# Up projection by Strassen's seven products, with part of its weight sums made by adding DMAs, and a down projection in two passes

## The chip, the cores and the metric

The kernel runs on one core of a Trainium2 chip. The core has five engines that take their instructions from queues of their own and in order: TensorE (PE in the profile; its weight loads are listed as PEld), VectorE (DVE), ScalarE (ACT), GpSimd (POOL) and SyncE (SP, which here only issues DMAs). The time is the device time of one execution in microseconds; lower is better. Runs of this kernel lie within about 0.2% of each other.

## The reference

One decoder block on a sequence of 512 tokens with D_MODEL = 2048, batch 1, everything float32:

```
mod = silu(c) @ w_ada + b_ada                      # six shift/scale/gate vectors
h   = rmsnorm(x) * (1 + sc1) + sh1
p   = h @ w_in                                     # input projection, 4384 columns
mix = concat(rwkv7_mixer(p[:, :3360]), pool_mixer(p[:, 3360:])) @ w_out
x   = x + gt1 * mix
h   = rmsnorm(x) * (1 + sc2) + sh2
u   = h @ w_up                                     # 2048 x 11264: 44 value and 44 gate tiles of 128
y   = causal depthwise conv of width 3 over u, plus bias
x   = x + gt2 * ((silu(y_gate) * y_value) @ w_down)   # 5632 x 2048
out = rmsnorm(x)
```

The change touches the last third: the second norm, `w_up`, the convolution, `w_down`. The rest keeps its arithmetic.

## The kernel before

Activations are kept transposed: channels on the 128 partitions, the 512 tokens along the free dimension. So a matrix of 2048 rows is 16 blocks of 128 (`KT`), and an output tile of 128 channels is one bank of the accumulation memory, 128 x 512 float32.

Every large matmul is made of three. A float32 operand is split into a high part, rounded to the fast format `F32R`, and a low part, the remainder; `mm3` (L111) then adds high x high, high x low and low x high into the same bank. Weights are split as they arrive: `split_weights` (L102) issues a DMA of 128 x 512 on SP (`wraw`, four buffers), ScalarE writes the high part (`whi`, L106), VectorE subtracts (`wlo`, L108; three buffers each). `project` (L116) runs this over the blocks of one output tile: 16 blocks for a tile of the up projection, 48 matmuls of 512 columns. The result of splitting activations lies in `ah`/`al` (L131) or, for the second norm, in `H2` (`hh`/`hl`).

Behind the two mixers the order of the work is as follows.

1. The output projection with `w_out` (L743 to L774). The last six output tiles are done in two halves of 256 tokens (`out_half`, L759), so that the second norm of the first half (`norm_rows`, `norm_bcast`, `second_norm`) can be computed while the second half is multiplied. Here GpSimd takes some of the weight splits.
2. `up_first` (L735): the first four column tiles of the up projection, block by block for one half of the tokens and then the other, with the rest of the second norm beside it.
3. Six groups of 8, 8, 8, 8, 4 and 8 pairs (`GROUPS`, L29). For each pair, `up_tile` (L813) makes a value and a gate tile, `conv` (L818) reads them from the bank (one ScalarE and two VectorE instructions each), then come Silu, a product, and `split_act`. When a group is complete, its activations are multiplied with the group's columns of `w_down` for all 16 output tiles, and added to the residual `x2` in SBUF (L848). In the first group VectorE also computes the 16 columns of the last gate (`ada_gate2`, L804), in four quarters each.
4. In the last group the output tiles 8 to 15 are again done in two halves (`down_half`, L856), with the final norm and the stores of the first half beside the second (L866 to L884).

The order of instructions on each engine comes from a scheduler in the framework, which places them by its own cost estimates and by dependences; the program order is its starting point. DMAs wait in the order in which SP issues them: a DMA that waits for its buffer holds up those behind it.

Of the kernel before, what the change touches and what calls it, by code (L numbers as in the profile page):

```python
# [16 lines left out]
P = 128  # L17
# [8 lines left out]
NWF = 8  # L26
Q = float(np.exp(-0.5))
WINS = (2, 4, 8, 16)
GROUPS = (8, 8, 8, 8, 4, 8)  # L29
# [25 lines left out]
def block_kernel(ctx, tc, a, out, stop=None, dbg=None):  # L55
# [4 lines left out]
    actp = ctx.enter_context(tc.tile_pool(name="act", bufs=1))  # L60
    wp = ctx.enter_context(tc.tile_pool(name="wts", bufs=2))
# [3 lines left out]
    cmat = cp.tile([P, 5, P], F32, tag="cmat", name="cmat")  # L65
    nc.sync.dma_start(cmat, a["cmat"][:, :, :])
    ident, bones, bmean, cent, ones = (cmat[:, i, :] for i in range(5))
    masks = cp.tile([P, 4, P], F32, tag="masks", name="masks")
    nc.sync.dma_start(masks, a["mask4"][:, :, :])
    mlev = cp.tile([P, 2, 64], F32, tag="mlev", name="mlev")  # L70
    nc.sync.dma_start(mlev, a["mlev"][:, :, :])
    scanm = cp.tile([P, NC, 129], F32, tag="scanm", name="scanm")
    nc.gpsimd.memset(scanm, 1.0)
    nc.gpsimd.memset(scanm[:, :, 0:1], 0.0)
    lanei = cp.tile([64, 16, 16], F32, tag="lanei", name="lanei")
    nc.sync.dma_start(lanei, a["lanei"][:, :, :])
    prec = cp.tile([P, 16], F32, tag="prec", name="prec")
# [33 lines left out]
    def mm3(ps, wh, wl, xh, xl, start, stop):  # L111
        PE.matmul(ps, wh, xh, start=start, stop=False)  # L112
        PE.matmul(ps, wh, xl, start=False, stop=False)  # L113
        return PE.matmul(ps, wl, xh, start=False, stop=stop)  # L114
# [575 lines left out]
    HT = T // 2  # L690

# [6 lines left out]

    def sumsq(acc, src, lo, hi, fresh):
        if fresh:  # L700
            S.activation(acc[:, lo:hi], src, AF.Square)
        else:
            t = rb.tile([P, T], F32, tag="h2", name="sqx", bufs=2)
            S.activation(t[:, lo:hi], src, AF.Square)
            V.tensor_add(acc[:, lo:hi], acc[:, lo:hi], t[:, lo:hi])

    H2 = [(rb.tile([P, T], F32R, tag=f"hh{k}", name=f"hh{k}"), rb.tile([P, T], F32R, tag=f"hl{k}", name=f"hl{k}"))
          for k in range(KT)]

    def residual(f, ps, gate, acc, lo, hi, fresh):  # L710

        V.scalar_tensor_tensor(x2[f][:, lo:hi], ps, gate, x2[f][:, lo:hi], op0=ALU.mult, op1=ALU.add)
        sumsq(acc, x2[f][:, lo:hi], lo, hi, fresh)
# [11 lines left out]
    def second_norm(hf, rstd, k):  # L725
        hs = slice(hf * HT, (hf + 1) * HT)
        t = rb.tile([P, T], F32, tag="h2", name="h2", bufs=2)[:, 0:HT]
        hi, lo = H2[k]
        modulate(hi[:, hs], lo[:, hs], t, x2[k][:, hs], rstd, gsc2[:, k : k + 1], mod[:, 48 + k : 49 + k])

    def up_first(hf, k):
        hs = slice(hf * HT, (hf + 1) * HT)
        wh, wl = split_weights(a["wup0"][k, :, :], G if hf == 0 and k % 2 else V)
        for i in range(4):
            sl = slice(i * P, (i + 1) * P)  # L735
            mm3(ups[i][:, hs], wh[:, sl], wl[:, sl], H2[k][0][:, hs], H2[k][1][:, hs], start=k == 0, stop=k == KT - 1)

    acc = rb.tile([P, T], F32, tag="acc", name="acc")
    x2 = []
    for k0 in range(4, KT, 4):  # L740
        for i in range(k0, min(k0 + 4, KT - 2)):
            load_mix(i)
        if k0 == KT - 4:  # L743
            M += last_mix
        for f in range(8):
            out_block(f, k0)
            if k0 == 8:
                for i in range(2):
                    t = rb.tile([P, T], F32, tag=f"x2_{2 * f + i}", name=f"x2_{2 * f + i}")
                    nc.sync.dma_start(t, a["xT"][:, 2 * f + i, :])  # L750
                    x2.append(t)
    for f in range(8):
        residual(f, pss[f], mod[:, 32 + f : 33 + f], acc, 0, T, f == 0)
    for f in range(8, NW):
        ps = bank()
        project(ps, a["wout"][f, :, :], M)
        residual(f, ps, mod[:, 32 + f : 33 + f], acc, 0, T, False)

    def out_half(hf, f, engs=(V,)):  # L759
        ps = bank()[:, 0:HT]  # L760
        project(ps, a["wout"][f, :, :], half(M, hf), engs=engs)
        residual(f, ps, mod[:, 32 + f : 33 + f], acc, hf * HT, (hf + 1) * HT, False)

    for f in range(NW, KT):
        out_half(0, f)
    for f in range(NW, KT):
        if f == NW + 1:
            dg = norm_rows(acc[:, 0:HT])
        if f == NW + 2:
            rstd0 = norm_bcast(dg)  # L770
        if f >= NW + 2:
            for k in range(3 * (f - NW - 2), 3 * (f - NW - 1)):
                second_norm(0, rstd0, k)
        out_half(1, f, (V, G) if f >= NW + 2 else (V,))  # L774

    ups = [bank() for _ in range(4)]
    for k in range(KT):
        if k + 12 < KT:
            second_norm(0, rstd0, k + 12)
        if k == 2:  # L780
            dg = norm_rows(acc[:, HT:T])
        if k == 5:
            rstd = norm_bcast(dg)
        if k >= 5:
            for k_ in range((k - 5) * 2, min((k - 4) * 2, KT)):
                second_norm(1, rstd, k_)
        up_first(0, k)
    for k in range(KT):
        up_first(1, k)
# [4 lines left out]
    def slot(i, dt=F32):  # L794
        return actp.tile([P, T], dt, tag=f"a{'hl'[i // 16]}{i % 16}", name="slot")

    cbs = []
    for i in range(4):
        t = slot(8 + i)
        nc.sync.dma_start(t, cact[0:1, i * T : (i + 1) * T].partition_broadcast(P))  # L800
        cbs.append(t)
    modg = cp.tile([P, 4, KT], F32, tag="modg", name="modg")

    def ada_gate2(j, after):  # L804
        for kq in range(4):
            wa = slot(12 + (4 * j + kq) % 4)
            nc.sync.dma_start(wa, a["ada2"][kq, 48 + j, :, :])
            jk = slot(24 + (4 * j + kq) % 2)
            with tc.issue_after(after.ins):
                V.scalar_tensor_tensor(jk, wa, 1.0, cbs[kq], op0=ALU.mult, op1=ALU.mult,  # L810
                                       accum_out=modg[:, kq, j : j + 1])

    def up_tile(n):  # L813
        ps = bank()
        project(ps, a["wup"][n, :, :], H2)
        return ps

    def conv(ps, j, tag):  # L818
        y = rb.tile([P, T], F32, tag=tag, name=tag, bufs=2)
        S.activation(y, ps, AF.Identity, bias=col("cb", j), scale=col("cw", 176 + j))  # L820
        V.scalar_tensor_tensor(y[:, 1:T], ps[:, 0 : T - 1], col("cw", 88 + j), y[:, 1:T], op0=ALU.mult, op1=ALU.add)
        V.scalar_tensor_tensor(y[:, 2:T], ps[:, 0 : T - 2], col("cw", j), y[:, 2:T], op0=ALU.mult, op1=ALU.add)
        return y

    j0 = 0
    for gi, gn in enumerate(GROUPS):
        A = []
        for jj in range(gn):
            j = j0 + jj
            yv = conv(ups[2 * j] if j < 2 else up_tile(2 * j), j, "t0")  # L830
            yg = conv(ups[2 * j + 1] if j < 2 else up_tile(2 * j + 1), 44 + j, "t1")
            S.activation(yg, yg, AF.Silu)
            after = V.tensor_mul(yv, yv, yg)
            A.append(split_act(jj, yv))
            if gi == 0 and jj >= 4:
                for i in range(4 * (jj - 4), 4 * (jj - 3)):
                    ada_gate2(i, after)
        if gi == 0:
            V.tensor_add(modg[:, 0, :], modg[:, 0, :], modg[:, 1, :])
            V.tensor_add(modg[:, 2, :], modg[:, 2, :], modg[:, 3, :])  # L840
            V.tensor_add(modg[:, 0, :], modg[:, 0, :], modg[:, 2, :])
            V.tensor_add(mod[:, 80:96], modg[:, 0, :], cols("b_ada", 80, 96))
        wsrc = a["wdn"][:, :, j0 * P : (j0 + gn) * P]
        if gi < len(GROUPS) - 1:
            for f in range(KT):
                ps = bank()
                project(ps, wsrc[f], A)
                V.scalar_tensor_tensor(x2[f], ps, mod[:, 80 + f : 81 + f], x2[f], op0=ALU.mult, op1=ALU.add)  # L848
        else:

            acc = rb.tile([P, T], F32, tag="acc", name="acc")

            def gate(f):
                return mod[:, 80 + f : 81 + f]

            def down_half(hf, f):  # L856
                ps = bank()[:, 0:HT]
                project(ps, wsrc[f], half(A, hf))
                residual(f, ps, gate(f), acc, hf * HT, (hf + 1) * HT, False)

            def finish(hf, k, rstd):
                hs = slice(hf * HT, (hf + 1) * HT)
                V.scalar_tensor_tensor(x2[k][:, hs], x2[k][:, hs], col("nf", k), rstd, op0=ALU.mult, op1=ALU.mult)  # L863
                nc.sync.dma_start(out[:, k, hs], x2[k][:, hs])
# [119 lines left out]
```

## Time and profile before

| what | value |
|---|---|
| median of three runs | 2449.82 us (2446.82 to 2450.76) |
| the profiled execution | 2452.14 us, of which the span from first to last instruction is 2450.0 |
| granted clock of TensorE, mean | 0.992 |
| busy: TensorE, VectorE, ScalarE, GpSimd | 2347.1, 1408.7, 874.6, 23.7 us |
| moved by DMA | 352.61 MB, mean 144 GB/s |

A group line of the profile reads: source line, engine, operation, output <- inputs, shapes, count | busy time in us, mean ns of one | idle time of the engine just before them, and who ended it. Busy times of matmuls overlap (their ends are modelled), so the cost of a matmul in a stream is read from the distance of starts or from counts in a window, not from its mean. A window line gives a stretch of time and each engine's busy time and count in it.

### The profile page before, as it was taken

How to read it: one execution, taken by the hardware profiler on the slowest of the kernel's cores; microseconds unless marked ns; L12 is line 12 of the kernel's file. 1: busy time of each engine (PE TensorE's matmuls, PEld its weight loads, DVE VectorE, ACT ScalarE, POOL GpSimd, SP SyncE). 2: the span in 40 equal slices, each digit the busy share in tenths (PEclk: the TensorE clock that was granted, in tenths of full speed). 3: DMA queues.
4: the chain of work that ended last, by engine and by line, in shares of the span. 5: the costliest groups of instructions: out<-in, count | busy, mean ns of one | idle time of the engine just before them, and what ended most of it. 6: DMA issues, size and time to landing. Idle time of an engine off the chain costs nothing.

```text
span 2450.0 us, 36089 instructions
## 1 busy us (share of the span) xinstructions
PE 2347.1 (96%) x13714; PEld 1872.0 (76%) x13714; DVE 1408.7 (57%) x2698; ACT 874.6 (36%) x1402; POOL 23.7 (1%) x29
## 2 busy tenths in 40 slices
PE   4889999999999999999999999999999999999997
PEld 3656666667667889887888888888888888888887
DVE  7987677787774357757534443444344434444457
ACT  3244443443433336532223322333233323323333
POOL 0000000000000002100000000000000000000000
PEclk9999999999999999999999999999999999999999
DMA  9975564556662635538533333333332333332335
GB/s 353 337 233 152 166 185 140 163 162 178 169 200 85 203 111 185 181 113 260 161 96 98 96 98 95 99 96 98 95 99 95 99 95 99 95 99 95 99 97 174
DMA packets 232160, 352.61 MB, mean 144 GB/s; under 512 B 74865, under 2 KB 80177, under 8 KB 227761
## 3 DMA queue, kind: packets, MB, share of 16 engines
q1 hardware_dynamic: 231986, 350.30, 46.0%
q8 instruction: 107, 1.75, 0.3%
q14 instruction: 67, 0.55, 0.1%
HBM read 334.22 MB, written 16.00 MB: 143 GB/s over the span
## 4 chain that ended last, share of the span: by engine, by line
PE 68%; DMA 3%; DVE 2%; ACT 1%; issue 0%; SPq 0%; POOL 0%; DVEq 0%; ACTq 0%; POOLq 0%
PE b L112 20%; PE b L114 20%; PE b L113 20%; DMA wraw<-wup 1%; PE mm L112 1%; PE mm L113 1%; PE mm L114 1%; DMA war<-ada 0%; PE pa L290 0%; DMA slot<-ada 0%; DMA wraw<-wdn 0%; DVE wlo L108 0%; DVE x L863 0%; PE pa L114 0%; PE pa L113 0%
## 5 line engine op out<-in xcount | busy, mean ns | idle before, releaser
L108 DVE TENSOR_TENSOR wlo<-wraw,whi 128x512 fp32r<-128x512 f32 x772 | 533.2, 692 | 694.9 <-ACT whi L106 679.6
L106 ACT CAST whi<-wraw 128x512 fp32r<-128x512 f32 x788 | 489.3, 622 | 1229.0 <-PE b L113 925.2
L114 PE MATMUL b<-hh,wlo 128*128 128x512 f32 (+1 forms) x1472 | 561.2, 381 | 5.9 <-DVE wlo L108 5.0
L112 PE MATMUL b<-hh,whi 128*128 128x512 f32 (+1 forms) x1472 | 560.0, 380 | 0.0
L113 PE MATMUL b<-hl,whi 128*128 128x512 f32 (+1 forms) x1472 | 559.5, 380 | 0.0
L112 PE MATMUL b<-ah,whi 128*128 128x512 f32 (+1 forms) x992 | 353.4, 357 | 4.3 <-ACT whi L106 2.5
L114 PE MATMUL b<-ah,wlo 128*128 128x512 f32 (+1 forms) x992 | 351.9, 355 | 0.8 <-DVE wlo L108 0.8
L113 PE MATMUL b<-al,whi 128*128 128x512 f32 (+1 forms) x992 | 352.1, 355 | 0.0
L114 PEld LDWEIGHTS b<-hh,wlo 128*128 128x128 f32 x1472 | 277.0, 188 | 62.1 <-DVE wlo L108 8.5
L112 PEld LDWEIGHTS b<-hh,whi 128*128 128x128 f32 x1472 | 276.9, 188 | 52.9 <-ACT whi L106 0.5
L113 PEld LDWEIGHTS b<-hl,whi 128*128 128x128 f32 x1472 | 277.0, 188 | 52.3
L112 PEld LDWEIGHTS b<-ah,whi 128*128 128x128 f32 x992 | 187.5, 189 | 33.7 <-ACT whi L106 4.3
L113 PEld LDWEIGHTS b<-al,whi 128*128 128x128 f32 x992 | 187.6, 189 | 27.4 <-DVE al L134 1.1
L114 PEld LDWEIGHTS b<-ah,wlo 128*128 128x128 f32 x992 | 187.6, 189 | 26.8 <-DVE wlo L108 1.2
L112 PE MATMUL mm<-ah,whi 128*128 128x512 f32 x464 | 192.4, 415 | 6.3 <-ACT upad L257 5.5
L113 PE MATMUL mm<-al,whi 128*128 128x512 f32 x464 | 191.8, 413 | 0.0
L114 PE MATMUL mm<-ah,wlo 128*128 128x512 f32 x464 | 190.1, 410 | 0.0
L343 DVE SCALAR_TENSOR_TENSOR jkr<-war,cq 128x512 bf16<-128x512 f32 x192 | 131.3, 684 | 18.7 <-DMA war<-ada 15.9
L848 DVE SCALAR_TENSOR_TENSOR x<-b,mod,x 128x512 f32<-128x512 f32 x80 | 59.7, 750 | 111.4 <-PE b L114 111.3
L112 PEld LDWEIGHTS mm<-ah,whi 128*128 128x128 f32 x464 | 88.4, 190 | 35.1 <-issue 10.4
L113 PEld LDWEIGHTS mm<-al,whi 128*128 128x128 f32 x464 | 88.3, 190 | 29.3 <-issue 13.0
L114 PEld LDWEIGHTS mm<-ah,wlo 128*128 128x128 f32 x464 | 88.4, 191 | 23.8 <-issue 6.3
(259 smaller groups left out, 2282.0 us busy)
## 6 DMA issues: line engine op xcount, KB each, us to landing
wraw<-wup SPq DMA_DIRECT2D x368, 256.0 KB, 3.0
war<-ada SPq DMA_DIRECT2D x192, 256.0 KB, 3.4
wraw<-wdn SPq DMA_DIRECT2D x192, 256.0 KB, 2.7
wraw<-win SPq DMA_DIRECT2D x140, 256.0 KB, 4.0
wa<-ada SPq DMA_DIRECT2D x32, 1024.0 KB, 6.9
wraw<-wout SPq DMA_DIRECT2D x88, 256.0 KB, 3.0
slot<-ada SPq DMA_DIRECT2D x64, 256.0 KB, 3.7
sp<-spill SPq DMA_DIRECT2D x21, 256.0 KB, 2.7
```

What stands on the lines that cost most here:

```text
L106: S.copy(hi, raw)
L108: eng.tensor_tensor(lo, raw, hi[:, :].bitcast(F32), op=ALU.subtract)
L112: PE.matmul(ps, wh, xh, start=start, stop=False)
L113: PE.matmul(ps, wh, xl, start=False, stop=False)
L114: return PE.matmul(ps, wl, xh, start=False, stop=stop)
L343: V.scalar_tensor_tensor(jk, wa, 1.0, cq[0], op0=ALU.mult, op1=ALU.mult, accum_out=modq[:, kq, j : j + 1])
L848: V.scalar_tensor_tensor(x2[f], ps, mod[:, 80 + f : 81 + f], x2[f], op0=ALU.mult, op1=ALU.add)
```

## The change

**Up projection.** The product of the 2048 rows of weights with the 512 tokens, for one pair (value tile, gate tile), is seen as a 2 x 2 by 2 x 2 block product: the blocks of the weights are two halves of the rows (8 blocks of 128) by value and gate; the blocks of the activations are the same halves of the rows by two halves of the tokens. Strassen's form (in Winograd's arrangement) makes seven block products of eight, with sums of weight blocks and of activation blocks before, and sums of results behind. One block product is 8 blocks x 3 matmuls of 256 columns (`product`).

The sums of the activations (`T1` to `T4`, and the plain blocks `Y11`, `Y21`, `Y22`) are made once, split, and kept in SBUF (`combos`, `split4`). The sums of the weights are needed for each of the 44 pairs: `r1` and `r3` are made by DMAs which GpSimd issues with `accum_op` add onto a table that another DMA has loaded; `r2` and `r4` by VectorE. Whole rows of `w_up` (128 x 2048, 1 MB) are loaded, into four buffers where the residual lay. For the first five pairs (`NB`) the two products that need only the first half of the tokens are made ahead (`first_two`), beside the second norm of the other half. The seventh product of a pair (`last_product`) follows the first of the next one. The convolution (`finish_pair`) now reads from SBUF, and the result is stored to DRAM (`ad`).

**Down projection.** Two passes over the 44 blocks, 22 each. Activations are loaded from DRAM and split (`act_pair`); the first pass's 16 results go to DRAM (`yd`); the residual, stored after the output projection (`x2d`), is loaded again in the second pass (`load_x2`). The second pass ends in two halves for the tiles 8 to 15, as before. The last gate's columns are computed in the first pass, from whole rows of 2048 (`ada3`). `w_up` is loaded as 128 x 1024 splits of its rows (`wsplit`), `w_down` as pieces of 8, 8 and 6 blocks.

**Output projection.** GpSimd no longer splits weights there; the four norms of the first half are done four blocks at a time (`normed`, `split4`); each finished tile is stored to DRAM. Pools are placed so that tables, weights and activations of the first stages can be freed before `ub` opens.

```diff
+    def product(ps, w, Y, start=True):
+        wh, wl = wsplit(w)
+        for k in range(8):
+            sl = slice(k * P, (k + 1) * P)
+            y = Y[k // 4]
+            mm3(ps, wh[:, sl], wl[:, sl], y[:, 0, k % 4, :], y[:, 1, k % 4, :], start=start and k == 0,
+                stop=k == 7, more=not start)
...
+    def first_two(n):
+        w = row(2 * n, ub, f"t4{n % 2}")
+        s_ = Slot("u1")
+        ps = bank()[:, 0:HT]
+        product(ps, w[:, W1], Y11)
+        S.copy(s_[:, H1], ps)
+        ps = bank()[:, 0:HT]
+        product(ps, w[:, W2], Y21)
+        V.tensor_add(s_[:, H0], s_[:, H1], ps)
+        ahead.append(s_)
...
+    t4 = []
+    for n in range(NB):
+        first_two(n)
+        if n == 0:
+            dg = norm_rows(acc[:, H1])
+        if n == 1:
+            rstd = norm_bcast(dg)
+        if 1 <= n < 5:
+            combos(n - 1)
...
+    def last_product(p):
+        j, u1, u2, b, w22, x = p
+        product(b, w22, T4, start=False)
+        if x is None:
+            S.copy(u2[:, H0], b)
+        else:
+            V.tensor_add(u2[:, H0], x[:, H0], b)
+            x.done()
+        finish_pair(j, u1, u2)
...
+    for j in range(NF):
+        w = []
+        for i in range(2):
+            w.append(row(2 * j + i, rb, f"x2_{rows % 4}"))
+            rows += 1
+        w11, w12, r1, w22 = w[0][:, W1], w[0][:, W2], w[1][:, W1], w[1][:, W2]
+        G.dma_start(r1, a["wup"][2 * j + 1, :, W2], accum_op=ALU.add)
+        r3 = wide("r3").rearrange("p a b -> p (a b)")
+        nc.sync.dma_start(r3, a["wup"][2 * j, :, W1])
+        G.dma_start(r3, a["wup"][2 * j + 1, :, W1], accum_op=ALU.add)
...
+            product(pa, w11, Y11)
+            S.copy(cap[:, H0], pa)
+            last_product(pend)
+            u1 = Slot("u1")
+            pb = bank()[:, 0:HT]
+            product(pb, w12, Y21)
+            V.tensor_add(u1[:, H0], cap[:, H0], pb)
...
+        product(pc, r1, T1)
+        S.copy(cap[:, H1], pc)
+        r2 = wide("r2").rearrange("p a b -> p (a b)")
+        V.tensor_add(r2, r1, w11)
+        product(pa, r2, T2, start=early)
...
+        r4 = wide("r4").rearrange("p a b -> p (a b)")
+        V.tensor_add(r4, r2, w12)
+        product(pc, r4, Y22, start=False)
+        V.tensor_add(u1[:, H1], cap[:, H0], pc)
...
+            product(pa, r3, T3, start=False)
+            V.tensor_add(u2[:, H1], cap[:, H1], pa)
...
+    def down(ps, f, h, acts):
+        for k0 in range(0, NJ, 8):
+            n = min(8, NJ - k0)
+            w = wide("wd").rearrange("p a b -> p (a b)")
+            nc.sync.dma_start(w[:, 0 : n * P], a["wdn"][f, :, (h * NJ + k0) * P : (h * NJ + k0 + n) * P])
+            wh, wl = wsplit(w[:, 0 : n * P])
...
+    for f in range(KT):
+        ps = bank()
+        down(ps, f, 0, A)
+        s_ = Slot("yd")
+        S.copy(s_.t, ps)
+        nc.sync.dma_start(yd[f], s_.t)
+        s_.done()
+        if f < 8:
+            ada_gate2(2 * f)
+            ada_gate2(2 * f + 1)
```

In the prediction P1 to P7 name the order of the products in a step: P1 with `w11`, P2 the previous pair's last product with `w22`, P3 with `w12`, P4 with `r1`, P5 with `r2`, P6 with `r4`, P7 with `r3`. `wide` has three buffers, which `r3`, `r2` and `r4` take in turn; `whi`/`wlo` of 1024 columns have three each.

More of the change, by code (lines that the diff above doesn't have):

```diff
@@ L690, in block_kernel @@
     HT = T // 2
+    H0, H1 = slice(0, HT), slice(HT, T)
+    QW = 4 * P
     def bank():
@@ L767, in block_kernel @@
         if f == NW + 1:
-            dg = norm_rows(acc[:, 0:HT])
+            dg = norm_rows(acc[:, H0])
         if f == NW + 2:
-            rstd0 = norm_bcast(dg)
+            rstd = norm_bcast(dg)
         if f >= NW + 2:
[L772 to L787, printed above, removed]
@@ L788, in block_kernel @@
-    for k in range(KT):
-        up_first(1, k)
+            n = f - NW - 2
+            q = (0, 2, 1, 3)[n]
+            normed(q, H0, rstd)
+            (Y11, Y21)[q // 2][q % 2] = split4(rb, f"y{q}", x2q[q][:, :, H0])
+        out_half(1, f)
+    hctx.close()
     if stop == "B":
         return
[L794 to L801, printed above, removed]
```

341 lines of the change are left out of this document (221 added, 120 removed).

## The prediction

> **What bounds the kernel now.** I read the page first, then windows over the stages behind the mixers, then the groups by shape, then the DMA issues.
>
> ```profile
> span 2450.0 us, 36089 instructions
> PE 2347.1 (96%) x13714; PEld 1872.0 (76%) x13714; DVE 1408.7 (57%) x2698; ACT 874.6 (36%) x1402; POOL 23.7 (1%) x29
> PE b L112 20%; PE b L114 20%; PE b L113 20%; DMA wraw<-wup 1%; PE mm L112 1%; PE mm L113 1%; PE mm L114 1%; DMA war<-ada 0%; PE pa L290 0%; DMA slot<-ada 0%; DMA wraw<-wdn 0%; DVE wlo L108 0%; DVE x L863 0%; PE pa L114 0%; PE pa L113 0%
> ...
> GB/s 353 337 233 152 166 185 140 163 162 178 169 200 85 203 111 185 181 113 260 161 96 98 96 98 95 99 96 98 95 99 95 99 95 99 95 99 95 99 97 174
> q1 hardware_dynamic: 231986, 350.30, 46.0%
> ```
>
> The chain that ended last is TensorE: 60% of the span lies in the three matmuls of the helper `mm3`. All data moves on one hardware queue; no row shows a DMA issued by GpSimd, nor one that adds.
>
> The windows give window, length, then busy time and count of PE, PEld, DVE, ACT, POOL, the granted clock, DMA share and GB/s. Behind them stand the first and the last of 48 consecutive half-width matmuls (start, modelled duration).
>
> ```profile
> 948.00:1100.00 152.00, 150.58 (x939) 135.52 (x938) 103.03 (x182) 76.61 (x137) 21.00 (x16) 1.00 0.50 154
> 1100.00:2385.00 1285.00, 1279.67 (x5629) 1055.54 (x5629) 588.18 (x918) 394.47 (x633) 0.00 (x0) 1.00 0.35 108
> 1500.00:2000.00 500.00, 500.00 (x2205) 413.27 (x2204) 213.42 (x308) 154.38 (x248) 0.00 (x0) 1.00 0.32 97
> ...
> 1017.74 0.28 PE L113 MATMUL b<-hl,whi 128*128 128x256 f32 x1
> ...
> 1023.38 0.28 PE L112 MATMUL b<-hh,whi 128*128 128x256 f32 x1
> ```
>
> From 948 us on, TensorE idles 1.4 us in the first window and 5.3 us in the second. So the stage is a number of matmuls times a pitch: 500.00/2205 = 0.2268 us for 512 columns; (1023.38 - 1017.74)/47 = 0.120 us for 256, which is 6% more than half. All at clock 1.00.
>
> The other engines' rows, which become terms below:
>
> ```profile
> L108 DVE TENSOR_TENSOR wlo<-wraw,whi 128x512 fp32r<-128x512 f32 x772 | 533.2, 692 | 694.9 <-ACT whi L106 679.6 <-PE mm L114 7.3 <-DMA war<-ada 2.0
> L204 DVE SCALAR_TENSOR_TENSOR jk<-wa,cb 128x2048 bf16<-128x2048 f32 x32 | 73.1, 2284 | 0.0
> L705 DVE TENSOR_TENSOR acc<-acc,sqx 128x256 f32<-128x256 f32 x28 | 11.7, 419 | 2.5 <-ACT sqx L704 2.5
> L396 DVE SCALAR_TENSOR_TENSOR inv<-rkv,vec,inv 128x512 f32<-128x512 f32 x8 | 6.0, 751 | 6.4 <-ACT inv L395 6.4
> L833 DVE TENSOR_TENSOR t<-t,t 128x512 f32<-128x512 f32 x44 | 30.1, 685 | 0.8 <-ACT t L832 0.8
> L712 DVE SCALAR_TENSOR_TENSOR x<-b,mod,x 128x256 f32<-128x256 f32 x28 | 13.5, 483 | 7.6 <-PE b L114 7.1
> ...
> L106 ACT CAST whi<-wraw 128x512 fp32r<-128x512 f32 x788 | 489.3, 622 | 1229.0 <-PE b L113 925.2 <-PE mm L113 125.0 <-issue 38.4
> L443 ACT ACTIVATE k<-al,drv,vec 128x512 f32<-128x512 f32 x8 | 6.5, 810 | 0.0
> L832 ACT ACTIVATE t<-t 128x512 f32<-128x512 f32 x44 | 27.6, 628 | 1.7 <-DVE t L822 1.7
> L522 ACT COPY tok<-pb 128x384 f32<-128x384 f32 x32 | 15.3, 479 | 48.4 <-PE pb L520 48.2
> L172 ACT ACTIVATE cb<-cb 128x2048 f32<-128x2048 f32 x1 | 1.9, 1909 | 8.6 <-DMA cb<-c 8.6
> ...
> wraw<-wup SPq DMA_DIRECT2D x368, 256.0 KB, 3.0
> wa<-ada SPq DMA_DIRECT2D x32, 1024.0 KB, 6.9
> DMA to landing us min/median/max: 4.9/6.9/13.9
> ```
>
> The last line belongs to `wa`, the only 1 MB weight loads.
>
> **Part by part. Matmuls.** Up projection before: 84 column tiles x 48 matmuls = 4032 x 0.2268 = 914.5, and 384 half-width ones in `up_first`, 46.1: 960.5 us. After: 44 pairs x 7 products x 24 = 7392 x 0.120 = 887.0. Gain 73.5. Seven eighths of the work would give 120, but all of it now runs at the half-width pitch. Down projection before: 1920 x 0.2268 + 384 x 0.120 = 481.5; after, the halved tiles have 22 blocks instead of 8: 1584 x 0.2268 + 1056 x 0.120 = 486.0, +4.5. Net -69.0.
>
> The Trainium skill, "TensorE: Matmul & The Clock Gate", section "Wait — 56ns, not 53.3ns?", puts the warm pitch at N/2.4 GHz plus 2.5 ns, 0.109 and 0.216 us; as an estimate by it the same counts would give -101. The trace disagrees (0.120 and 0.2268); the rows decide, and I give that result no chance of its own.
>
> **A steady step** (one pair j from 5 on; seven products P1..P7 of 2.88 us; 20.16 us). Between 512 and 2048 columns VectorE needs 692 and 2284 ns: 1.22 us for 1024. ScalarE, from 622 and 1909: 1.05. VectorE per step: 7 low parts 8.5, the two sums left to it (`r2`, `r4`) 2.4, three half adds at 0.42, four conv steps at 0.75, one product 0.69: 15.9 us. ScalarE: 7 high parts 7.4, two conv activations at 0.81, Silu 0.6, four half copies at about 0.4 (384 columns take 0.48): 11.2 us. Both fit. With three weight buffers a split may start two products ahead, so I put the order of the instructions on a timetable by these durations: each low part is ready about 3 us before its product. Cost nothing, covered by TensorE; if that cover went, the step would be VectorE's.
>
> **The adding DMAs** are the open price. GpSimd issues 88 (44 on `r1`, 44 on `r3`), 512 KB each; on GpSimd nothing else waits behind them but the next of them. In the changed order, VectorE computes `r2` of pair j+1 *ahead* of the low part of P7 of pair j. So this ring decides: P2's low part frees row 2j-1; SP loads row 2j+3 into it (1 MB, time L); GpSimd adds onto `r1` (X); then `r2`, P7's low part, `r4`, P1's low part, a half add and P2's low part follow on VectorE, 5 x 1.22 + 0.42 = 6.5, with semaphores 6.7. TensorE sees nothing while L + X is below 20.16 - 6.7 = 13.5 us; above, every step grows by the excess. L: 4.9 to 6.9, its row; I take 6, as the previous `r3` add runs beside it. X: it reads what 1 MB reads (table and destination). Below it lies a plain 512 KB load, about 3.6 between 3.0 for 256 KB and 4.9 for 1 MB; above, two 1 MB transfers one after the other in a loaded queue, 13.8. I take 6.5, nearest to the 1 MB row. L + X = 12.5: inside, by 1 us. Ends 8.5 and 20.7, that is 0 to 7.2 us a step. A gain is excluded, the step being TensorE's already. `r3` has a looser ring (load 3.6, add, split; about 12 us of room).
>
> The Trainium skill, "Collectives: The Full Stack", section "The bandwidth ceiling: the fold count and why AG ≠ RS ≠ AR", says that an adding DMA loses nothing by the addition, and half its rate by reading two sources. With the fit in "DMA: Bandwidth & Descriptors", section "Anatomy of one DMA — SWDGE (gpsimd) path" (2.0 us plus bytes over 436 GB/s), X would be 4.4 as an estimate, and the sum as without stalls. No row here shows it.
>
> **Traffic.** A step moves 2 MB rows, 0.5 + 1.0 MB for the sums and a 0.25 MB store: 3.75 MB in 20.16 us, 186 GB/s against 97 now; the first slices of the page reach 353. On SP the 44 `ad` stores wait for the pair's last product with the next rows behind them, but stand in the order behind `r3`, when their data is long there. Nothing.
>
> **The start.** `first_two` gives TensorE 10 products, 28.8 us. VectorE has 32 operations of 1024 columns there (10 low parts, 22 for norms, differences and splits): 39, plus adds and norm 3. My timetable, from the end of the out projection: first row issued late (behind two `x2d` stores on SP), TensorE starts 1.7 us late; two waits for VectorE, 4.4; the products end at 35. The quarter buffer for row 1 is free at 45, row and add 12.5 later with 1.05 for the high part: product T1 starts at 59. TensorE idle: 30 us, 1.4 in the window before: +28.6. Ends: 18 (L + X 8.5, VectorE never waiting) and 40.
>
> In `out_half` GpSimd no longer splits and VectorE gets four norms: per tile 4 x 0.69 + 0.48 + 0.42 + 2 x 1.22 = 6.1 against 48 x 0.120 = 5.76: +1.5 for four (0 to 4). The 26 `x2d` stores on SP have weight loads behind them, four buffers ahead: nothing.
>
> Pairs 0 to 4 have five products, 14.4 us, but the same rows: their ring (2.9 + L + X = 15.4, and VectorE's waits behind it) is longer. I find three waits of about 3 us on T3: +10 (0 to 35).
>
> **Into the down projection.** 22 activation tiles come back from DRAM (22 x 0.69 on VectorE, 22 x 0.62 on ScalarE), with four gate rows (2.28 each), the last conv and the first weight splits: from P7's low part on, VectorE has some 33 us to the last tile's split, against 24 us of TensorE: +10 (3 to 15). The gates leave the first pairs, where their waits were the 5.3 us of the second window: -5.3. The second pass loads into three free buffers and then follows the first, buffer by buffer: nothing; the 16 `yd` and 32 reload DMAs on SP lie within the 15 us a tile takes.
>
> **Sum:** -69.0 + 28.6 + 1.5 + 10 + 10 - 5.3 = -24: span 2426, and with the 2.1 us that the profiled run (2452.14) has beside its span, 2428. The median shown, 2449.82, is 2.3 below that run; I leave this in the range.
>
> **Rivals.**
> 1. *The adding DMA sets the step* (slower). Its place is `r2` on VectorE waiting for `r1`; it decides above L + X of about 14.0, since 0.55 us x 44 steps eat the 24. At 15.0: 44 x 1.5 = 66 more, 2494; at 16, 2538; at the upper end, 2745. For it: GpSimd has no DMA row yet, and my margin is 1 us. Against it: the bytes.
> 2. *VectorE sets the step*: 15.9 us busy in a strict order with ScalarE between. If waits bring it to 21 us: 0.84 x 39 = 33, 2461. For: 79% busy; against: 3 us lead per product.
> 3. *The seams cost less*: VectorE overlaps the start (18) and the handover (3): 2410, and with the early pairs at nothing 2400.
> That the change saves no TensorE work is excluded by the counts; that its pitch takes half the saving back is in the sum.
>
> **How the numbers follow.** Forecast 0.43 (2428; its own range 2410 to 2452), rival 1 0.40, rival 2 0.10, rival 3 0.07. Within 0.2% (2445 to 2455, about what can be told from no change) fall 0.03 of the forecast, 0.02 of rival 1 and 0.01 of rival 2. Faster 0.40 + 0.07 = 0.47, same 0.06, slower 0.38 + 0.09 = 0.47. Range 2405 to 2540: below lies most of rival 3, above the third of rival 1 with L + X over 16.
>
> **What would show it.** Right: half-width matmuls at 0.120; a period of 20.2 us per pair; `r1` landing within 6 to 7 us of its issue; a TensorE gap of some 24 us before the first T1; some 10 us at the handover. Wrong: a period above 20.5, with VectorE's idle time before `r2` put down to a DMA (rival 1), or VectorE over 95% busy (rival 2).

## The result, and the profile after

The changed kernel takes 2559.02 us (median of four runs, 2535.93 to 2571.86) against 2450.29 us before: ratio 1.0436, 95% interval 1.0348 to 1.0524. It is slower by about 109 us, where the prediction had 22 us less. Its four runs are far apart, and their order is that of the mean granted clock: 2535.93 us at 0.974, 2547.82 at 0.965, 2570.21 at 0.958, 2571.86 at 0.956. The profiled run is the first of these; its span is 2534.2 us.

The page of the changed kernel, in the lines that answer to those of before (span, busy times, clock in 40 slices):

```profile
span 2534.2 us, 42335 instructions
PE 2319.7 (92%) x17026; PEld 1998.0 (79%) x17026; DVE 1639.3 (65%) x2621; ACT 1038.2 (41%) x1466; POOL 78.8 (3%) x101
...
PEclk9999999999999999799999999999999999999988
...
```

TensorE is busy for 27 us less than before, in a span 84 us longer. The clock's row has two weak places: slice 17, where the up projection starts, and the last two slices, the end of the down projection's second pass. Windows by stage say more (start and end, length, then busy time and count of PE, PEld, DVE, ACT, POOL, granted clock, DMA share, GB/s):

```profile
975.00:1035.00 60.00, 30.68 (x248) 29.84 (x247) 40.45 (x43) 30.37 (x44) 2.73 (x3) 0.80 0.55 169
1035.00:1110.00 75.00, 63.69 (x472) 62.11 (x473) 54.70 (x68) 31.79 (x37) 6.04 (x7) 0.91 0.76 211
1200.00:1400.00 200.00, 200.00 (x1670) 200.00 (x1669) 150.95 (x170) 104.10 (x139) 17.25 (x20) 1.00 0.70 197
2200.00:2300.00 100.00, 86.26 (x329) 66.94 (x330) 23.06 (x24) 16.22 (x20) 0.00 (x0) 0.91 0.25 73
2300.00:2400.00 100.00, 77.06 (x486) 70.01 (x486) 34.90 (x40) 25.50 (x32) 0.00 (x0) 0.92 0.39 110
2400.00:2480.00 80.00, 58.38 (x416) 55.77 (x416) 32.19 (x49) 20.47 (x26) 0.00 (x0) 0.89 0.46 138
2480.00:2534.00 54.00, 32.16 (x238) 30.24 (x237) 20.60 (x36) 10.08 (x14) 0.00 (x0) 0.87 0.35 107
```

The third row is the Strassen stage in its steady part: TensorE without a pause, 200.00/1670 = 0.1198 us a matmul. The first two rows are the start, whose idle time (29.3 and 11.3 us) the prediction had. The last four are the second pass: TensorE idles for 14, 23 and 27% of the first three windows and 40% of the last, which holds the tail; no other engine is busy for more than some 40%, the DMAs for less than half of the time, and the clock is 0.87 to 0.92. The prediction had put that pass at nothing beyond its matmuls.

Where its time goes shows in the timelines of ScalarE, VectorE and TensorE at one tile boundary there (start, duration; in brackets the idle time before and who ended it):

```profile
2240.20 0.63 ACT L731 ACTIVATE sqx<-x 128x512 f32<-128x512 f32 x1 [14.94 <-DVE x L737]
2240.74 1.98 ACT L837 CAST uhi<-wd 128x1024 fp32r<-128x1024 f32 x2
2244.78 0.83 ACT L837 CAST uhi<-wd 128x768 fp32r<-128x768 f32 x1 [2.06 <-DMA wd<-wdn]
2260.56 0.63 ACT L731 ACTIVATE sqx<-x 128x512 f32<-128x512 f32 x1 [14.96 <-DVE x L737]
```

```profile
2239.36 0.75 DVE L737 SCALAR_TENSOR_TENSOR x<-b,mod,x 128x512 f32<-128x512 f32 x1 [13.10 <-PE b L123]
...
2259.72 0.75 DVE L737 SCALAR_TENSOR_TENSOR x<-b,mod,x 128x512 f32<-128x512 f32 x1 [13.12 <-PE b L123]
```

```profile
2259.29 0.39 PE L123 MATMUL b<-act,ulo 128*128 128x512 f32 x1
2262.18 0.50 PE L121 MATMUL b<-act,uhi 128*128 128x512 f32 x1 [2.50 <-ACT uhi L837]
2262.52 0.40 PE L122 MATMUL b<-act,uhi 128*128 128x512 f32 x1
2263.44 0.50 PE L123 MATMUL b<-act,ulo 128*128 128x512 f32 x1 [0.53 <-DVE ulo L839]
...
2266.30 0.63 PE L121 MATMUL b<-act,uhi 128*128 128x512 f32 x1
2266.72 0.63 PE L122 MATMUL b<-act,uhi 128*128 128x512 f32 x1
...
2267.42 0.40 PE L121 MATMUL b<-act,uhi 128*128 128x512 f32 x1
```

On ScalarE the square of tile f (`sqx`, L731) stands *ahead* of the first weight split of tile f+1 (`uhi`, L837). The square waits for the residual on VectorE (L737), and the residual for the last matmul of tile f. So ScalarE stands still for 14.94 us, and only then splits weights that could have been split long before: last matmul, residual, square, split, next matmul. TensorE idles for 2.50 us, then 0.53 for the low part; then the ten matmuls from 2263.44 to 2267.42 take 3.98 us, most of them 0.43 us apart, where 0.2268 each would be 2.27. The tile takes 2259.72 - 2239.36 = 20.36 us where its 66 matmuls need 14.97.

The program does name the square ahead of the next tile's loads and splits, but no dependence holds back the first two of these splits, and the scheduler is free to place them earlier: in the first pass it put all three splits of a tile ahead of the copy that ends the tile before. What is new is where `sumsq` puts its square:

```diff
-            t = rb.tile([P, T], F32, tag="h2", name="sqx", bufs=2)
+            t = wide("sqx")[:, 0:2, :].rearrange("p a b -> p (a b)")
```

`wide` is the ring of three buffers from which `down` takes its three weight pieces per tile (`wd`). Four things now take turns in three buffers, so the third piece of tile f+1 gets the buffer that the square of tile f leaves.

### The profile page after: what moved, and what is told of

Same layout as the page of the kernel before. It is cut to its first block, busy times and chain, and to the rows that moved or that the text cites. A ratio compares the mean times of both kernels' runs of the same rounds, so it can differ in the third digit from the quotient of the medians.

```text
span 2534.2 us, 42335 instructions
## 1 busy us (share of the span) xinstructions
PE 2319.7 (92%) x17026; PEld 1998.0 (79%) x17026; DVE 1639.3 (65%) x2621; ACT 1038.2 (41%) x1466; POOL 78.8 (3%) x101
## 4 chain that ended last, share of the span: by engine, by line
PE 74%; DVE 11%; DMA 7%; issue 3%; ACT 3%; SPq 1%; POOL 0%; ACTq 0%; DVEq 0%; POOLq 0%
PE b L123 18%; PE b L121 18%; PE b L122 18%; PE mm L122 3%; PE mm L121 3%; PE mm L123 3%; DVE jk L213 3%; DMA wrow<-wup 2%; DVE ulo L839 2%; DMA war<-ada 1%; ACT uhi L837 1%; PE pb L538 1%; PE pb L536 1%; DMA al<-ad 1%; DMA wraw<-win 1%
## 5 line engine op out<-in xcount | busy, mean ns | idle before, releaser
L121 PE MATMUL b<-t,uhi 128*128 128x256 f32 x1408 | 401.3, 285 | 30.2 <-ACT uhi L837 28.4
L123 PE MATMUL b<-t,ulo 128*128 128x256 f32 x1408 | 401.0, 285 | 10.1 <-DVE ulo L839 10.1
L122 PE MATMUL b<-t,uhi 128*128 128x256 f32 x1408 | 400.5, 284 | 0.0
L121 PE MATMUL b<-act,uhi 128*128 128x512 f32 (+1 forms) x880 | 319.7, 363 | 58.4 <-ACT uhi L837 54.8
L123 PE MATMUL b<-act,ulo 128*128 128x512 f32 (+1 forms) x880 | 319.4, 363 | 15.9 <-DVE ulo L839 15.9
L122 PE MATMUL b<-act,uhi 128*128 128x512 f32 (+1 forms) x880 | 317.6, 361 | 0.4 <-DVE act L1016 0.4
L121 PE MATMUL b<-y,uhi 128*128 128x256 f32 x1056 | 297.7, 282 | 2.4 <-ACT uhi L837 2.4
L122 PE MATMUL b<-y,uhi 128*128 128x256 f32 x1056 | 298.7, 283 | 0.0
L123 PE MATMUL b<-y,ulo 128*128 128x256 f32 x1056 | 298.4, 283 | 0.0
L121 PEld LDWEIGHTS b<-t,uhi 128*128 128x128 f32 x1408 | 272.5, 194 | 31.6 <-ACT uhi L837 28.9
L837 ACT CAST uhi<-wrow 128x1024 fp32r<-128x1024 f32 x176 | 184.3, 1050 | 254.5 <-PE b L122 233.2
L123 PEld LDWEIGHTS b<-t,ulo 128*128 128x128 f32 x1408 | 272.3, 193 | 11.3 <-DVE ulo L839 11.3
L122 PEld LDWEIGHTS b<-t,uhi 128*128 128x128 f32 x1408 | 272.2, 193 | 0.0
L114 ACT CAST whi<-wraw 128x512 fp32r<-128x512 f32 x228 | 140.7, 619 | 295.3 <-PE mm L122 125.4
L116 DVE TENSOR_TENSOR wlo<-wraw,whi 128x512 fp32r<-128x512 f32 x228 | 156.0, 688 | 118.7 <-ACT whi L114 101.3
L837 ACT CAST uhi<-wd 128x1024 fp32r<-128x1024 f32 (+1 forms) x120 | 114.7, 973 | 219.5 <-PE b L122 170.0
L837 ACT CAST uhi<-r 128x1024 fp32r<-128x1024 f32 x132 | 138.8, 1051 | 156.2 <-PE b L122 153.4
```

The costliest lines, as they stand in the source:

```text
L114: S.copy(hi, raw)
L116: eng.tensor_tensor(lo, raw, hi[:, :].bitcast(F32), op=ALU.subtract)
L121: PE.matmul(ps, wh, xh, start=start, stop=False, skip_group_check=more)
L122: PE.matmul(ps, wh, xl, start=False, stop=False, skip_group_check=more)
L123: return PE.matmul(ps, wl, xh, start=False, stop=stop, skip_group_check=more)
L837: S.copy(hi[:, 0:n], src)
```

## Experiments

My theory after this: the shared ring made the scheduler place the square ahead of the next tile's splits, and this order, with the clock that the gaps cost, is the whole miss. The rivals: the second pass is bound by its loads; the lower clock is a cause and not a result; and, for the rest of the kernel, the two remaining rivals of the prediction (adding DMA, VectorE).

**A buffer of its own for the square (own_buffer).**

```diff
-            t = wide("sqx")[:, 0:2, :].rearrange("p a b -> p (a b)")
+            s_ = sqslot()          # Slot("sqx") in the second pass, else None
+            t = s_.t if s_ else wide("sqx")[:, 0:2, :].rearrange("p a b -> p (a b)")
             S.activation(t[:, lo:hi], src, AF.Square)
             V.tensor_add(acc[:, lo:hi], acc[:, lo:hi], t[:, lo:hi])
+            if s_:
+                s_.done()
```

> Edit: in the second pass of the down projection the square of a finished tile gets a 2 KB slot of its own instead of a turn in the ring of three wide buffers that the weight pieces use; nothing else is touched. Theory (queue order): the changed kernel loses its time because ScalarE's and VectorE's queues hold square and residual of tile f ahead of the weight split of tile f+1, and the shared ring is what put them in that order. Then the tile period of the second pass falls from 20.36 us to that of the first pass, 15.2 us, and that of a half tile from about 11.95 us to 8.0 us: 8 x 5.2 + 15 x 3.9 + some 8 at the norm = about 108 us off the profiled 2536 us, so about 2428 us, 0.99 of the kernel before. Rival (loads): a tile's three loads come late because 1.41 MB per half tile is more than the queue brings in 8 us; then full tiles reach 15.2 us but half tiles stay above 9.5 us, and the time is 2450 to 2465 us. Rival (clock): the lower granted clock is the cause and not the result of the gaps; then the gaps close but matmuls in the second pass still show some 0.42 us at 512 columns, and the time stays above 2480 us.

Measured: 2437.74 us (2433.23 to 2441.35), 0.9955 of the kernel before (0.9941 to 0.9969); I had about 2428. The windows of the second pass, and ScalarE's timeline over a tile boundary:

```profile
2200.00:2300.00 100.00, 100.00 (x464) 82.94 (x464) 33.95 (x38) 24.95 (x28) 0.00 (x0) 1.00 0.36 105
2300.00:2400.00 100.00, 100.00 (x836) 99.94 (x835) 59.65 (x83) 41.89 (x54) 0.00 (x0) 1.00 0.69 205
```

```profile
2247.58 0.84 ACT L845 CAST uhi<-wd 128x768 fp32r<-128x768 f32 x1 [3.00 <-PE b L122]
2248.60 0.63 ACT L737 ACTIVATE sqx<-x 128x512 f32<-128x512 f32 x1 [0.18 <-DVE x L745]
...
2262.76 0.84 ACT L845 CAST uhi<-wd 128x768 fp32r<-128x768 f32 x1 [3.00 <-PE b L122]
2263.77 0.64 ACT L737 ACTIVATE sqx<-x 128x512 f32<-128x512 f32 x1 [0.18 <-DVE x L745]
```

The order has turned: the split of the next tile at 2247.58 stands ahead of the square at 2248.60, and the splits now wait only for a split buffer that TensorE frees (`PE b L122`). TensorE has no idle time, the clock is 1.00. Full tiles take 2263.77 - 2248.60 = 15.17 us, half tiles 7.91. From the last copy of the first pass to the last residual it is 2420.80 - 2170.43 = 250.4 us, against 2519.23 - 2166.89 = 352.3 in the changed kernel: 102 us come back, from an edit of one buffer. The waits of TensorE there, in the changed kernel, were these:

```profile
PE b L121 <- ACT uhi L837: 53.8, 22, 8.0
PE b L123 <- DVE ulo L839: 14.2, 22, 0.8
```

That is 68 us of the 102. The other 34 are busy time: the same 1588 matmuls are busy for 282.9 us in the changed kernel and for 248.9 here. By the distances of their starts, some 27 of the 34 are matmuls that follow each other more slowly; the other 7 lie at the edges of the waits, where no next matmul overlaps the end of the last. The loads' rival is refuted (7.91 us a half tile at 205 GB/s), and so is a clock that is low of itself.

**The splits ahead by program order, the ring still shared (split_ahead).** This tells the order from the number of buffers.

```diff
+    nxt = [prep(0, 1)]                 # prep: the three loads and splits of one tile
...
-        down(ps, f, 1, A)
+        down(ps, f, 1, A, nxt.pop())   # its matmuls alone
+        ahead_of(0, f)                 # nxt.append(prep(f + 1, 1))
         residual(f, ps, gate(f), acc, 0, T, f == 0)
```

> Edit: the ring stays shared, but the program loads and splits the weights of tile f+1 ahead of the residual and the square of tile f. Theory (queue order): with the splits ahead in the queues the shared ring costs little, since the square then takes a buffer whose piece was split a tile ago; period 15.2 us for full tiles and 8 to 8.5 us for half tiles, 2428 to 2440 us. Rival (ring): three buffers for four allocations are too few in whatever order; the loads of the next tile wait for the square, and full tiles stay above 17 us and half tiles above 10 us, 2480 us or more.

Measured: 2450.9 us (2441.62 to 2457.24), ratio 1.0007 (0.9995 to 1.0019). Full tiles are 15.17 us apart, as with the own buffer; but half tiles are not 7.91 us apart, by their residuals in VectorE's timeline:

```profile
2334.37 0.48 DVE L737 SCALAR_TENSOR_TENSOR x<-b,mod,x 128x256 f32<-128x256 f32 x1
2343.33 0.48 DVE L737 SCALAR_TENSOR_TENSOR x<-b,mod,x 128x256 f32<-128x256 f32 x1
2351.86 0.48 DVE L737 SCALAR_TENSOR_TENSOR x<-b,mod,x 128x256 f32<-128x256 f32 x1
```

8.5 to 9.0 us each: ScalarE's splits there wait 1.7 to 2.9 us for `wd`, whose load starts late. So the order was nearly everything; with the ring still shared, 13 us are left (2450.9 - 2437.7). By the two profiles some 8 of them lie in the half tiles, where a tile is too short to hide the ring, and 4 in the first tile of the pass, where TensorE waits 4.0 us for an activation that comes back from DRAM. Half of my expectation was right: it had 2428 to 2440.

**TensorE kept busy in the gaps (filler).** The changed kernel, with matmuls that serve nothing behind each tile of the second pass.

```diff
         down(ps, f, 1, A)
+        filler(A, 12)      # 12 matmuls of 512 columns into an unread bank; 24 of 256 behind a half tile
         residual(f, ps, gate(f), acc, 0, T, f == 0)
```

> Edit: the changed kernel as it is, with matmuls that serve nothing (12 of 512 columns behind each full tile, 24 of 256 columns behind each half tile, into a bank that nobody reads) in the second pass, placed where TensorE stands idle between two tiles. They shorten no wait; they only keep TensorE busy in it. Theory (the gaps lower the clock): a full tile of 20.36 us is 14.97 us of matmuls at 0.2268 us, about 3.0 us of waiting, and 2.3 us of matmuls at the halved clock; with the filler the clock is not lowered, the period falls to 18.0 to 18.4 us and that of half tiles to 11.0 to 11.6 us, in all 15 to 28 us less than without. Rival (the slow matmuls have another cause, such as the splits that run beside them): the period stays at 20.4 us or grows by the filler's surplus, and the time does not fall.

Measured: 2519.18 us (two runs, 2515.87 and 2522.49), ratio 1.029 (1.0271 to 1.0309): more work, and less time than the changed kernel's fastest run by 17 us. Profile against profile it is 13 us less (2535.93 - 2522.49), just short of the 15 to 28 that I had. TensorE's timeline at a boundary:

```profile
2240.96 1.97 PE L1066 MATMUL b<-act 128*128 128x512 f32 x8
2243.62 0.50 PE L121 MATMUL b<-act,uhi 128*128 128x512 f32 x1 [0.69 <-ACT uhi L837]
...
2244.19 1.09 PE L1066 MATMUL b<-act 128*128 128x512 f32 x4
2245.11 0.40 PE L123 MATMUL b<-act,ulo 128*128 128x512 f32 x1
2245.35 0.39 PE L121 MATMUL b<-act,uhi 128*128 128x512 f32 x1
```

The chain residual, square, split is as long as before, but the matmuls behind it keep their 0.23 us. The period of a full tile falls from 20.36 to 18.90 us (I had 18.0 to 18.4), that of half tiles from about 11.95 to 11.28. The granted clock between 2200 and 2400 us is 1.00, where the changed kernel has 0.91 and 0.92. So the slow matmuls come from TensorE's own idle time.

The Trainium skill, "TensorE: Matmul & The Clock Gate", section "HAM oscillation — how this bites in real kernels", puts the idle time that halves the clock at more than about 3.4 us. Here 2.50 us and, after two matmuls, another 0.53 were enough in each of the six full tiles that follow such a wait; the measurement decides. The length of the gap does not settle it alone, though. The half tiles of the changed kernel have gaps of 2.02 and 0.76 us, and only every second one is slowed: their residuals (2345.23, 2357.92, 2369.13 us) are 12.69 and 11.21 us apart in turn, and two windows of equal length and equal busy time hold 79 matmuls at one clock and 91 at the other.

```profile
2491.00:2505.00 14.00, 11.22 (x79) 10.81 (x78) 4.23 (x5) 3.13 (x4) 0.00 (x0) 0.88 0.51 149
2505.00:2519.00 14.00, 11.22 (x91) 10.80 (x90) 4.23 (x5) 3.13 (x4) 0.00 (x0) 1.00 0.11 31
```

What decides which gaps lower the clock is not shown.

**Both sums by VectorE (vector_sums).** The other new mechanism undone, on top of own_buffer.

```diff
-        G.dma_start(r1, a["wup"][2 * j + 1, :, W2], accum_op=ALU.add)
         r3 = wide("r3").rearrange("p a b -> p (a b)")
-        nc.sync.dma_start(r3, a["wup"][2 * j, :, W1])
-        G.dma_start(r3, a["wup"][2 * j + 1, :, W1], accum_op=ALU.add)
+        V.tensor_add(r3, w11, r1)
+        V.tensor_add(r1, r1, w22)
```

> Edit: own_buffer, and both sums of weight quarters that the accumulating DMAs make are made by VectorE instead, from the two rows that are loaded anyway; the pool queue and three of five loads' worth of traffic per pair are gone. By the prediction's sum VectorE goes from 15.1 us to 15.1 + 2 x 1.2 = 17.5 us of a steady pair of 20.1 us, and the accumulating DMAs were hidden there: steady pairs stay at 20.1 us. At the start the first pair's matmuls wait for an accumulating DMA that was issued at 1025.8 us and landed at 1034.9 us in the profile of the changed kernel; a sum by VectorE takes 1.2 us, so 6 to 8 us less there: 6 to 8 us below own_buffer in all. Rival (VectorE sets the step): at 17.5 of 20.1 us queue order makes TensorE wait for low parts, pairs go to 21 us or more, 39 x 0.9 = 35 us above own_buffer. Rival (the start is bound by the combinations): no difference to own_buffer within 2 us.

Measured: 2415.66 us (2411.51 to 2416.5), ratio 0.9864 (0.985 to 0.9877): 22 us less than own_buffer, three times what I had. The windows of own_buffer, then of vector_sums:

```profile
975.00:1035.00 60.00, 34.00 (x274) 32.97 (x272) 44.01 (x47) 33.30 (x49) 1.87 (x2) 0.84 0.53 178
1035.00:1110.00 75.00, 61.37 (x455) 60.00 (x456) 50.95 (x63) 30.85 (x36) 6.91 (x8) 0.89 0.74 200
```

```profile
975.00:1035.00 60.00, 37.78 (x276) 36.66 (x275) 49.98 (x51) 33.50 (x46) 0.00 (x0) 0.78 0.45 156
1035.00:1110.00 75.00, 74.47 (x612) 73.86 (x611) 72.59 (x91) 37.91 (x46) 0.00 (x0) 0.99 0.40 145
1200.00:1400.00 200.00, 200.00 (x1670) 200.00 (x1670) 167.71 (x189) 106.00 (x139) 0.00 (x0) 1.00 0.32 119
```

In the steady part nothing changes: 1670 matmuls in 200 us with VectorE at 84% instead of 75%. So VectorE does not set the step even with 1.7 us more a pair. Between 1035 and 1110 us, the pairs 0 to 4, the 13.6 us of idle time are 0.5, and the clock rises from 0.89 to 0.99.

**The same for pairs 0 to 4 alone (early_sums).** The diff is that of vector_sums under `if j < 5`.

> Edit: own_buffer, with the two sums made by VectorE for the pairs 0 to 4 alone, and by accumulating DMAs for the other 39. vector_sums was 22 us below own_buffer; this tells whether the 22 us lie in the first pairs or are spread over the 39 steady ones. Theory (latency at the seam: row, then accumulating DMA, then split, with five products a pair to hide them instead of seven): the whole gain is there, 2414 to 2420 us, and the stretch from the end of the out projection to pair 5 is as short as in vector_sums. Rival (the traffic of the accumulating DMAs slows something in the steady pairs or behind them): only a part of the 22 us, 2425 us or more.

Measured: 2419.2 us (2416.42 to 2427.3), ratio 0.9884 (0.9859 to 0.9908). 18.5 of the 22 us lie in the first five pairs. The other 3.5 are no more than what the stage ahead differs by in the two profiles (its last residual starts at 979.32 us here, at 975.78 in vector_sums). So in the other 39 pairs the adding DMA is hidden, and so are VectorE's sums.

**The adding DMA doubled (add_twice).** Own_buffer; r1 then holds its second quarter twice.

```diff
         G.dma_start(r1, a["wup"][2 * j + 1, :, W2], accum_op=ALU.add)
+        G.dma_start(r1, a["wup"][2 * j + 1, :, W2], accum_op=ALU.add)
```

> Edit: own_buffer, and the accumulating DMA onto r1 is issued twice, so that r1 holds its second quarter doubled (a changed product; only its time is of interest). This prices the ring of the prediction: row load L, accumulating DMA X, and 6.7 us of VectorE behind it have to fit into 20.16 us. The profile of the changed kernel has L at 4.8 and X at 5.5 us; with 2 X it is 4.8 + 11.0 + 6.7 = 22.5 us, 2.3 us too long. Theory (the ring decides): steady pairs go from 20.1 to about 22.4 us, 39 x 2.3 = 90 us, and some 20 us more in the first pairs, 2530 to 2560 us, with VectorE waiting for r1 ahead of r2. Rival (there is more room in it than the prediction's order has, since the scheduler can put other work of VectorE ahead): steady pairs stay under 20.6 us, and only the first pairs lose, 2450 to 2475 us.

Measured: 2605.01 us in one run, 167 us above own_buffer, and more than the 2530 to 2560 that I had. Rows of its window and of VectorE's timeline (L981 is `r2`, which reads r1):

```profile
1200.00:1400.00 200.00, 180.37 (x1401) 178.20 (x1400) 125.08 (x142) 88.31 (x118) 21.57 (x25) 0.93 0.72 191
```

```profile
1409.18 1.23 DVE L981 TENSOR_TENSOR r<-wrow 128x1024 f32<-128x1024 f32 x1 [5.47 <-issue]
...
1479.73 1.23 DVE L981 TENSOR_TENSOR r<-wrow 128x1024 f32<-128x1024 f32 x1 [5.94 <-issue]
```

Between these two lie two more; so a steady pair takes (1479.73 - 1409.18)/3 = 23.5 us, or 23.9 on the mean of 37 pairs (I had 22.4), which makes some 148 of the 167 us. VectorE idles for some 6 us just ahead of `r2`. The row gives no releaser but "issue"; that it is r1 follows from the edit, which is all that differs, and from GpSimd's timeline: there the second addition is issued at 1474.07 us, 5.7 ahead of the `r2` at 1479.73. The ring of the prediction gives, with this profile's medians between 1200 and 1900 us, a row load of 4.8, twice 5.7 for the adding DMA and 6.7 of VectorE: 22.9 us. The ring exists where I had put it, and decides as soon as it is longer than the pair.

**The gap at the start (row_buffers, seven_ahead).** On top of vector_sums:

```diff
-            w.append(row(2 * j + i, rb, f"x2_{rows % 4}"))
+            w.append(row(2 * j + i, rb, f"x2_{(0, 2, 1, 3)[rows % 4]}"))
```

and for seven_ahead also `NB = 7` for `NB = 5`.

> Edit: vector_sums, and the rows of the pairs take the four quarter buffers in the order 0, 2, 1, 3 instead of 0, 1, 2, 3, so that the first pair's two rows need the two buffers that the second combination step releases, and not one of the third step. In the profile of vector_sums TensorE is idle for 19.4 us before the first pair, and its second row lands at 1024.3 us. Theory (the first pair waits for its row's buffer): the row comes some 6 us earlier, the wait falls to 12 to 15 us, and the time to 2408 to 2412 us. Rival (VectorE, which works without a pause there, sets the end of the gap): no change within 2 us, 2414 to 2417 us.

> Edit: row_buffers, and seven pairs instead of five have their first two products ahead of the combinations, so that TensorE has 11.5 us more to do in the gap. Each pair moved costs VectorE 2.8 and ScalarE 2.5 us there. Theory: the gap shrinks by 11.5 us of products and grows by 5.6 us of VectorE's work, 5 to 6 us less than row_buffers. Rival (slots): seven of eleven slots are then taken at the first pair, finished halves wait for slots, and the first pairs lose more than that: 0 to 10 us above row_buffers.

Measured: row_buffers 2416.26 us (ratio 0.9863, 0.9843 to 0.9882), no different from vector_sums: the longest wait of TensorE fell from 19.4 us to 17.8 only. My expectation failed. In this run VectorE no longer waits for a row, and from 1024.88 us to the splits of the first pair it works without a pause: the rival, VectorE's work on the combinations, sets the end of the gap. seven_ahead 2410.76 us (2407.15 to 2413.07), ratio 0.9842 (0.9825 to 0.986), 5.5 us less by the medians, as worked out, and its four runs all lie below the four of row_buffers (2413.72 to 2419.93): more TensorE work inside the gap does help. It is the fastest version here, 38 us under the kernel before. Its windows of the start:

```profile
975.00:1035.00 60.00, 50.44 (x374) 48.51 (x372) 50.88 (x56) 38.54 (x55) 0.00 (x0) 0.91 0.55 193
1035.00:1110.00 75.00, 71.84 (x568) 70.94 (x569) 72.94 (x89) 37.57 (x44) 0.00 (x0) 0.95 0.40 143
```

## Why the prediction was wrong, step by step

- **The step that failed** is the sentence on the second pass: "loads into three free buffers and then follows the first, buffer by buffer: nothing". I looked at the loads only. The second pass is not the first: behind each tile it has a residual and a square in place of a copy, and the square sits in the same three buffers. By the profiles this cost 102 us, 68 of waiting and 34 of busy time, most of it at the lower clock; own_buffer, which undoes that alone, brings them back. (By the medians the difference between the two kernels is 121 us; no trace shows where the 19 beyond the 102 lie.) No rival named this either: the time is one that rival 1 would have given, but by another mechanism, and the range's upper end, 2540, came from the adding DMA. The order of the instructions on ScalarE, which I used for the steady step, would have shown it here.
- **Matmuls, -69:** right. 0.1198 us for 256 columns where I had 0.120. The half-width pitch takes 46.5 of the 120 us back, rather less than the "half" behind the rivals. A full tile of the down projection takes 15.17 us, not 66 x 0.2268 = 14.97: 0.2 x 24 = 5 us missed. The estimate by the pitch of the Trainium skill, "TensorE: Matmul & The Clock Gate", section "Wait — 56ns, not 53.3ns?", comes to -104 by the same counts, not -101; it enters no other term.
- **The steady step at 20.16 us:** right (20.1). VectorE's 150.95 us in 200 make 15.2 a pair (15.9 predicted), ScalarE's 104.10 make 10.5 (11.2). The DMAs move 197 GB/s; my 186 took the megabyte of the rows, 1024 KB, for a million bytes.
- **Rival 1, the adding DMA sets the step (0.40):** refuted for this kernel, and its mechanism shown by add_twice. Measured by the rows below, over all pairs, X is 5.6 us for r1 (`wrow` from GpSimd's queue; `r` is the table of r3) and L 4.8, so that L + X is 10.4, not 12.5, and the margin 3 us, not 1: X lies between the estimate of 4.4 and my 6.5. In the window from 960 to 1110 us, which has the first five pairs, X is 8.9 (the last row).

```profile
wrow<-wup SPq DMA_DIRECT2D x93, 1024.0 KB, 4.8
...
r<-wup SPq DMA_DIRECT2D x44, 512.0 KB, 4.0
r<-wup POOLq DMA_DIRECT2D x44, 512.0 KB, 5.5
wrow<-wup POOLq DMA_DIRECT2D x44, 512.0 KB, 5.6
```

```profile
wrow<-wup POOLq DMA_DIRECT2D x5, 512.0 KB, 8.9
```

- **Rival 2, VectorE sets the step (0.10):** refuted, even at 84% (vector_sums).
- **The start, +28.6, and pairs 0 to 4, +10:** the sizes were right, 29.3 us of idle time between 975 and 1035 us and 11.3 behind. The path is the one that I had, the row's buffer, the row and the adding DMA, as the rows below show; but that the size came out is in part luck. The buffer was free 42.7 us after the output projection's last residual (1017.95 - 975.26) instead of 45, and then the row took 7.3 us and the addition 9.1, 16.4 instead of 12.5. With the DMA out of the way it is VectorE that ends the gap (row_buffers). The waits of pairs 0 to 4 are those of the adding DMAs and of the load that `r3` needs (early_sums). What I left out is the clock behind the gap: 248 + 472 matmuls need 720 x 0.12 = 86.4 us and were busy for 94.4, 8 us more, most of it at a slower pitch.

```profile
1025.82 0.87 POOL L948 DMA_DIRECT2D wrow<-wup  x1 [3.21 <-DMA wrow<-wup]
1034.90 1.05 ACT L837 CAST uhi<-wrow 128x1024 fp32r<-128x1024 f32 x1 [11.23 <-DMA wrow<-wup]
1035.99 0.58 PE L121 MATMUL b<-t,uhi 128*128 128x256 f32 x1 [27.91 <-ACT uhi L837]
```

- **Handover, +10:** 6.6 us of idle time between 1900 and 1950 us, inside 3 to 15.
- **Half tiles of the output projection, +1.5:** the last residual there starts at 975.26 us against 974.04 before, in bounds; but in other executions of the same code it is 979.84 (own_buffer) or 983.48 us (row_buffers), outside of them. That this stage has become so variable is seen and not explained.
- **The gates, -5.3:** no run tells this term from the others.

Put together: own_buffer is the changed kernel as the prediction had imagined it, and measured 2437.7 against 2428. The clock behind the gap (8), the pitch of the down projection (5) and the output projection's last tiles (979.84 - 974.04 - 1.5 = 4) add 17 us, the handover gives back 4 (5.7 us idle there): 13 against the 10 measured, so the account closes to some 3 us. So the mechanisms of the Strassen stage held, with their sizes in the sum if not each by itself, and the forecast fell by a stage to which I had given one sentence.

## What to carry to other kernels

A small temporary that takes its buffer from a ring of streamed weights can turn the order of a whole stage: look, for each stage that a change touches, at the order of consumer and next producer on every queue, also where no work was added. Price a repeated gap on TensorE above its length; in this kernel waits of 68 us in all cost another 34 us of TensorE's time. The adding DMAs were free here where a full step covered row, addition and split in sequence, and cost 18.5 us in the five shorter pairs at the start; there VectorE's sums were the better choice.

## What the runs showed of the hardware that I had not expected

- Idle times of 2.50 and 0.53 us, with two matmuls between them, lower TensorE's clock: from 1.3 to 5.2 us after the restart, ten matmuls of 512 columns take 3.98 us instead of 2.27. With filler matmuls in the gap, leaving 0.69 us idle, nothing of this is seen at such a boundary. Gaps of 2.02 and 0.76 us, between half tiles, do it every second time.
- A DMA that adds 512 KB onto a table in SBUF lands 5.5 us after its issue (r3; 5.6 for r1), beside 4.0 us for a plain load of 512 KB in the same stage: a factor of 1.4. In the first five pairs, r1's takes 8.9. The Trainium skill, "Collectives: The Full Stack", section "The bandwidth ceiling: the fold count and why AG ≠ RS ≠ AR", has half the rate for the two reads of the addition in a ReduceScatter; these rows are latencies of a DMA on one core, and show less than that. Issued twice onto the same bytes, 512 KB take 5.7 us each, and GpSimd issues the second only when the first has landed.
